# Feed-forward weight sums of pairs 1 to 5: added by GpSimd in place of VectorE

## The chip, the cores and the metric

The kernel runs on one core of a Trainium2 chip, in one launch. The metric is the device time of that core in microseconds (us); a lower time is better. Engines are named as in the profile: PE is TensorE (matmuls), PEld its weight loads, DVE is VectorE, ACT is ScalarE, POOL is GpSimd and SP is SyncE, which here only issues DMAs.

## The reference, cut to what matters

The reference is a two-layer streaming encoder on 512 tokens of width 1024, all in float32. Each layer has a mixer, a cross-attention to a memory and a gated feed-forward; a last RMSNorm ends it. The change lies in the feed-forward, which both layers have:

```python
D_FF = 256 * math.ceil(8 * D_MODEL / 3 / 256)   # 2816

def conv_ffn(xn, w_up, conv_w, conv_b, w_down):
    h = causal_depthwise_conv(xn @ w_up, conv_w) + conv_b
    g, u = jnp.split(h, 2, axis=-1)
    return (jax.nn.gelu(g) * u) @ w_down

x = x + conv_ffn(rms_norm(x, ffn_norm[layer]), ffn_w_up[layer], ffn_conv_w[layer], ffn_conv_b[layer], ffn_w_down[layer])
```

## The kernel before

**Tiling.** Tokens lie along the free dimension (512 columns), features on the 128 partitions. The product xn @ w_up has 44 blocks of 128 output features. Block p (of g) and block 22 + p (of u) form pair p, so each layer has 22 pairs, 0 to 21. Products are done in three matmuls of a high and a low part (`mm3`, lines 291 to 293: high by high, low by high, high by low), so every weight is split: ACT casts it to the high part (`wh`), DVE subtracts that from the original to get the low part (`wl`, all at line 282).

**Plain pairs and pairs of seven products.** Pair 0 goes through `plain`: two blocks of 24 matmuls on 512 columns. Pairs 1 to 21 (the tuple `SEVEN`) go through `seven`, a Strassen-like scheme with seven products of 12 matmuls on 256 columns instead of eight. It multiplies four forms of the tokens (made once per layer by `forms`, kept in `kv` tiles) and parts of the weights. Its weights per pair are: `f3`, the block of g as it is loaded (tile `raw`, 1024 columns); `f1`, the tile `sa`, where SP loads half of each block and a second DMA from POOL adds the block of u onto it in SBUF (line 1732, `accum_op=ALU.add`); `a22`, a part of u's block (tile `ra`, 512 columns); and two sums that an engine has to add. S2 = `sa[512:] + raw[:512]` goes to a tile `sb` (line 1753). After S2 has been split, S4 = `sb + raw[512:]` is added in place (line 1759) and split too. `sb` has two buffers, `sa` and `raw` three each.

**Behind the products.** The results are combined into `hs` (ACT copies at 1803 and 1810, DVE subtractions at 1793; ACT also keeps two intermediate results `u` at 1790 and seeds a PSUM bank at 1786). DVE then multiplies by the normalizer `rb` (1816). `tail` makes the convolution of three taps (ACT at 1669, DVE twice for each half at 1676), the gelu (ACT 1684), the product of g and u (DVE 1686) and the split of the activations (ACT 1690, DVE 282).

**The down projection.** w_down is taken in five chunks of pairs. From pair 5 on, `fill` puts two blocks `down` of a chunk that is ready into each pair: each is 12 matmuls on 512 columns with its own weight (tile `dr`) to be split. Pairs 1 to 4 have none, so there PE has the least work for each operation of DVE and ACT.

**What sets the order.** Nothing in the feed-forward is issued where it is written. `add(engine, duration, function, dependencies, due, take, free)` gives a task to the planner `Sched`, with a cost that is written into the program and a due time counted in PE time (`clock`). `Sched.run` goes through the tasks in the order of the costs and due times; each engine's queue is what comes out, and each engine works its queue in that order. S2's add is due 5 us before its pair, S4's 1.5 us before; splits are due 2 to 3 us before (plus an offset by product). For DVE the cost of 512 columns is `tt(512)`, 0.598 us. POOL has in this part of the program the accumulating DMAs and two small memsets of `hs`.

Of the kernel before, what the change touches and what calls it, by code (L numbers as in the profile page):

```python
# [14 lines left out]
ALU = mybir.AluOpType  # L15
# [50 lines left out]
class Plan:  # L66
# [11 lines left out]
    def add(self, fn, dur=0.0, deps=(), prio=None, take=(), free=(), chain=(), pre=(), after=0.0, order=(), load=(), st=None):  # L78
        it = Item(fn, dur, [d for d in deps if d is not None], len(self.items) if prio is None else prio, take, free, chain, pre, after, order, load, st)
        it.n = len(self.items)  # L80
        self.items.append(it)
        return it
# [154 lines left out]
class Builder:  # L237
# [1269 lines left out]
    def ffn_steps(self, layer, mp):  # L1507
# [3 lines left out]
        nc, t = self.nc, self.t  # L1511
        sc = Sched(raw=3, h=3, s2=1, s4=1, a22=1, sa=3, sb=2, ra=2, hs=2, c=1, dr=2, u2=1, u5=1, act=10, acc=2, y=2, s=2, w=2)
        add = sc.add
        tt = lambda n: 0.055 + 1.06e-3 * n
# [17 lines left out]
        def raw_tile(st, tag):  # L1532
            pool, n, bufs = RAWS[tag]
            st[tag] = self.til(pool, tag, (P, n), bufs=bufs)
            return st[tag]

        def load(st, tag, src, cols, at, dur=0.0017):
            def fn():
                to = raw_tile(st, tag)[:, :cols]
                nc.sync.dma_start(to.rearrange("p (a b) -> p a b", a=2) if len(src.shape) == 3 else to, src)  # L1540

            return add("SP", dur * cols, fn, (), at, [(tag, st)], (), 4.0)

        def parts(st, off=0):
            st["wh"], st["wl"] = self.parts(off)
# [177 lines left out]
        def seven(p, fill):  # L1723
            st, sa, sb, r2, f1, f3, s2, s4, a22 = ({} for _ in range(9))
            at = clock[0]
            A1, A2 = t["up"][layer, p], t["up"][layer, 22 + p]
            tt_ = nc.vector.tensor_tensor
            up2 = t["up"][layer].rearrange("(j p) r c -> p r j c", j=2)


            def onto(out, src, cols, deps, due):
                return add("POOL", 0.0029 * cols, lambda: nc.gpsimd.dma_start(out(), src(), accum_op=ALU.add), deps, due, (), (), 6.0)  # L1732

            SB = lambda: sb["sb"][:]
            soon = 40.0 if p < 5 else 0.0
            b1 = load(sa, "sa", up2[p][:, :, :512], 1024, at - 20.0 - soon, 0.0 if soon else 0.0017)
            b1 = onto(lambda: sa["sa"][:], lambda: A2, 1024, [b1], at - 16.0 - soon)
            l2 = load(r2, "raw", A1, 1024, at - 12.0)
            l1 = load(a22, "ra", A2[:, 512:], 512, at - 6.0)

            def small(s, tag):
                s["wh"], s["wl"] = small_(tag)

            def split(s, cols, deps, due, alloc, take, raw, free=()):
                def hi():
                    alloc()
                    nc.scalar.copy(s["wh"][:, :cols], raw())  # L1747

                h = add("ACT", act(cols), hi, deps, due - 3.0, take)
                return add("DVE", tt(cols), lambda: self.sub(s["wl"][:, :cols], raw(), s["wh"][:, :cols]), [h], due - 2.0, (), free)  # L1750

            def s2_():
                tt_(out=raw_tile(sb, "sb")[:], in0=sa["sa"][:, 512:], in1=r2["raw"][:, :512], op=ALU.add)

            b2 = add("DVE", tt(512), s2_, [b1, l2], at - 5.0, [("sb", sb)])
            w3 = split(f3, 1024, [l2], at, lambda: parts(f3, OFF), [("h", f3)], lambda: r2["raw"][:])
            w2 = split(s2, 512, [b2], at, lambda: small(s2, "s2"), [("s2", s2)], SB)
            w1 = split(f1, 1024, [b1], at + 1.0, lambda: parts(f1, OFF), [("h", f1)], lambda: sa["sa"][:])
            b4 = add("DVE", tt(512), lambda: tt_(out=SB(), in0=SB(), in1=r2["raw"][:, 512:], op=ALU.add), [w2], at - 1.5)
            w22 = split(a22, 512, [l1], at + 4.0, lambda: small(a22, "a22"), [("a22", a22)], lambda: a22["ra"][:], [("ra", a22)])  # L1760
            w4 = split(s4, 512, [b4], at + 5.0, lambda: small(s4, "s4"), [("s4", s4)], SB, [("sb", sb)])
            joined([w1, b2], at, [("sa", sa)])
# [533 lines left out]
```

## Time and profile before

| what | value |
|---|---|
| median of 3 runs | 1458.25 us (1457.26 to 1460.52) |
| the profiled execution | 1458.17 us |
| its span, first to last instruction | 1456.4 us |
| granted TensorE clock, mean | 0.999 |
| accumulating DMAs of the feed-forward on POOL | 42, 855 ns each to issue |
| pairs 1 to 5, layer 0 | about 417 to 475 us of the span |
| pairs 1 to 5, layer 1 | about 1120 to 1178 us of the span |

A row of the timeline has the start, the duration, the engine, the line, the operation, the tile written and the tiles read with their sizes, and in brackets how long the engine sat idle before it and what ended that. Consecutive operations on DVE overlap by some 0.08 us, so the distance of two starts, and not the duration, tells what one costs a gapless stream. A row of the waits has the time in total, how often, and the longest.

### The profile page before, as it was taken

What the parts mean: (1) busy time and instruction counts of PE and PEld (TensorE: products, weight loads), DVE (VectorE), ACT (ScalarE), POOL (GpSimd) and SP (SyncE); (2) the same over time, 40 slices, a digit from 0 to 9 for tenths busy, and PEclk for the clock granted to TensorE, in tenths of its full rate; (3) what the DMA queues carried; (4) which work ended last, traced back from release to release, by engine and by line L of the source; (5) the groups of instructions that cost most, each with busy time, mean ns of one, the idle gap of its engine ahead of it and who ended that gap; (6) DMA issues with size and microseconds to landing.
All of it is one profiled execution on the core that took longest, in us unless ns stands there. A gap on an engine that the chain in (4) does not pass through costs nothing.

```text
span 1456.4 us, 24072 instructions
## 1 busy us (share of the span) xinstructions
PE 1441.7 (99%) x9019; PEld 1279.8 (88%) x9019; DVE 1225.6 (84%) x2223; ACT 986.1 (68%) x1776; POOL 73.3 (5%) x116
## 2 busy tenths in 40 slices
PE   9999999999999999999999999999999999999998
PEld 7888787998899999999888888889988999999987
DVE  7789987867899988889669988887779998888974
ACT  7689666655677777777547665566566777777764
POOL 0001120000000000000000100000000000000000
PEclk9999999999999999999999999999999999999999
DMA  5222336752246666562233332656414666666422
GB/s 200 87 74 73 117 119 199 171 177 88 94 128 163 183 158 161 150 163 74 84 101 109 109 110 65 204 142 189 131 48 119 160 179 172 156 160 156 105 67 79
DMA packets 70628, 190.24 MB, mean 131 GB/s; under 512 B 7520, under 2 KB 7520, under 8 KB 70512
## 3 DMA queue, kind: packets, MB, share of 16 engines
q1 hardware_dynamic: 62736, 162.17, 35.1%
q0 software_dynamic: 7200, 26.22, 10.7%
q8 instruction: 70, 1.15, 0.3%
q14 instruction: 46, 0.38, 0.1%
q10 hardware_dynamic: 576, 0.33, 0.1%
HBM read 186.56 MB, written 2.13 MB: 130 GB/s over the span
## 4 chain that ended last, share of the span: by engine, by line
PE 82%; DVE 10%; ACT 4%; issue 2%; DMA 1%; POOL 0%; DVEq 0%; SPq 0%; POOLq 0%; ACTq 0%
PE acc L291 15%; PE acc L292 15%; PE acc L293 14%; PE w L293 6%; PE w L291 6%; PE w L292 6%; PE s L293 3%; PE s L291 3%; PE s L292 3%; PE acc L352 2%; PE acc L354 2%; PE acc L353 2%; DVE wl L282 2%; DMA sa<-in_xq_dram 1%; DVE x L771 1%
## 5 line engine op out<-in xcount | busy, mean ns | idle before, releaser
L282 DVE TENSOR_TENSOR wl<-raw,wh 128x1024 fp32r<-128x1024 f32 (+3 forms) x181 | 213.9, 1182 | 41.2 <-ACT wh L285 32.3
L291 PE MATMUL acc<-xh,wh 128*128 128x256 f32 (+1 forms) x624 | 206.8, 331 | 0.1
L293 PE MATMUL acc<-xh,wl 128*128 128x256 f32 (+1 forms) x624 | 205.7, 330 | 0.1
L292 PE MATMUL acc<-xl,wh 128*128 128x256 f32 (+1 forms) x624 | 205.5, 329 | 0.0
L285 ACT CAST wh<-raw 128x1024 fp32r<-128x1024 f32 (+1 forms) x123 | 126.6, 1034 | 84.6 <-PE acc L292 43.0
L1676 DVE SCALAR_TENSOR_TENSOR c<-hs,vec,c 128x512 f32<-128x512 f32 x176 | 130.5, 749 | 15.9 <-ACT c L1669 14.0
L291 PEld LDWEIGHTS acc<-xh,wh 128*128 128x128 f32 x624 | 117.2, 188 | 12.1 <-ACT v L1917 0.6
L293 PEld LDWEIGHTS acc<-xh,wl 128*128 128x128 f32 x624 | 117.1, 188 | 12.0 <-DVE wl L282 0.5
L292 PEld LDWEIGHTS acc<-xl,wh 128*128 128x128 f32 x624 | 117.2, 188 | 11.5
L293 PE MATMUL w<-ah,wl 128*128 128x512 f32 x304 | 119.1, 392 | 0.0
L292 PE MATMUL w<-al,wh 128*128 128x512 f32 x304 | 118.6, 390 | 0.0
L291 PE MATMUL w<-ah,wh 128*128 128x512 f32 x304 | 118.5, 390 | 0.0
L282 DVE TENSOR_TENSOR wl<-sa,wh 128x1024 fp32r<-128x1024 f32 x52 | 63.6, 1222 | 17.0 <-ACT wh L1747 15.6
L1669 ACT ACTIVATE c<-hs,vec 128x512 f32<-128x512 f32 x88 | 71.2, 816 | 9.6 <-DVE hs L1816 8.2
L1747 ACT CAST wh<-sa 128x1024 fp32r<-128x1024 f32 x42 | 44.0, 1049 | 35.4 <-PE w L292 30.4
L293 PEld LDWEIGHTS w<-ah,wl 128*128 128x128 f32 x304 | 57.1, 188 | 12.0
L291 PEld LDWEIGHTS w<-ah,wh 128*128 128x128 f32 x304 | 57.1, 188 | 10.0 <-ACT w L1584 0.2
L292 PEld LDWEIGHTS w<-al,wh 128*128 128x128 f32 x304 | 57.0, 188 | 9.8
L282 DVE TENSOR_TENSOR s<-sb,s 128x512 fp32r<-128x512 f32 x92 | 63.1, 686 | 2.2 <-ACT s L285 0.3
L1554 ACT CAST wh<-dr 128x512 fp32r<-128x512 f32 x64 | 39.7, 621 | 34.1 <-PE w L292 32.2
L1732 POOL DMA_DIRECT2D sa<-in_up_dram x42 | 35.9, 855 | 515.7 <-DMA sa<-in_up_dram 173.9
L291 PE MATMUL acc<-mem,wh 128*128 128x256 f32 (+1 forms) x192 | 61.5, 320 | 0.0
(534 smaller groups left out, 4667.8 us busy)
## 6 DMA issues: line engine op xcount, KB each, us to landing
raw<-in_up_dram SPq DMA_DIRECT2D x46, 512.0 KB, 3.5
sa<-in_up_dram SPq DMA_DIRECT2D x42, 512.0 KB, 4.3
sa<-in_up_dram POOLq DMA_DIRECT2D x42, 512.0 KB, 5.7
dr<-in_down_dram SPq DMA_DIRECT2D x64, 256.0 KB, 2.7
ra<-in_up_dram SPq DMA_DIRECT2D x42, 256.0 KB, 3.0
raw<-in_xk_dram SPq DMA_DIRECT2D x16, 512.0 KB, 3.6
raw<-in_wo_dram SPq DMA_DIRECT2D x16, 512.0 KB, 3.5
raw<-in_xv_dram SPq DMA_DIRECT2D x16, 512.0 KB, 3.4
```

The source lines that it names most:

```text
L282: self.nc.vector.tensor_tensor(out=lo, in0=v, in1=hi.bitcast(F32), op=ALU.subtract)
L285: self.nc.scalar.copy(hi, v)
L291: mm(out, wh, xh, start=first, stop=False, skip_group_check=parts)
L292: mm(out, wh, xl, start=False, stop=False, skip_group_check=parts)
L293: mm(out, wl, xh, start=False, stop=last, skip_group_check=parts)
L352: mm(ps, xh[k][:, ts], wh[:, ws], start=(k == 0), stop=False)
L353: mm(ps, xh[k][:, ts], wl[:, ws], start=False, stop=False)
L1554: nc.scalar.copy(st["wh"][:, :cols], st[tag][:, :cols])
L1669: nc.scalar.activation(st["c_"][:, j, :], hs()[:, j, 2:514], AF.Identity, scale=self.col("cw", (layer * 3 + 2) * 44 + blk), bias=self.col( ...
L1676: nc.vector.scalar_tensor_tensor(out=c, in0=hs()[:, j, n : n + 512], scalar=w, in1=c, op0=ALU.mult, op1=ALU.add)
L1732: return add("POOL", 0.0029 * cols, lambda: nc.gpsimd.dma_start(out(), src(), accum_op=ALU.add), deps, due, (), (), 6.0)
L1747: nc.scalar.copy(s["wh"][:, :cols], raw())
```

## The change

In pairs 1 to 5 of each layer the two adds S2 and S4 are issued on GpSimd (`nc.gpsimd.tensor_tensor`), and the planner is told that each takes 1.8 us there. In all other pairs they stay on VectorE. Operands, tiles and buffers are the same.

```diff
             tt_ = nc.vector.tensor_tensor
+            by_, add_ = (("POOL", 1.8), nc.gpsimd.tensor_tensor) if p in (1, 2, 3, 4, 5) else (("DVE", tt(512)), tt_)
...
             def s2_():
-                tt_(out=raw_tile(sb, "sb")[:], in0=sa["sa"][:, 512:], in1=r2["raw"][:, :512], op=ALU.add)
-
-            b2 = add("DVE", tt(512), s2_, [b1, l2], at - 5.0, [("sb", sb)])
+                add_(out=raw_tile(sb, "sb")[:], in0=sa["sa"][:, 512:], in1=r2["raw"][:, :512], op=ALU.add)
+
+            b2 = add(*by_, s2_, [b1, l2], at - 5.0, [("sb", sb)])
...
-            b4 = add("DVE", tt(512), lambda: tt_(out=SB(), in0=SB(), in1=r2["raw"][:, 512:], op=ALU.add), [w2], at - 1.5)
+            b4 = add(*by_, lambda: add_(out=SB(), in0=SB(), in1=r2["raw"][:, 512:], op=ALU.add), [w2], at - 1.5)
```

The added line moves the later ones down by one, so 1732 becomes 1733, 1753 becomes 1754, 1759 becomes 1760, 1793 becomes 1794 and 1816 becomes 1817 in the kernel after. As the planner has other costs, it also orders the tasks around the adds anew.

On POOL, at the start of layer 0's feed-forward, the queue before reads as follows (`sa` are the accumulating loads of pairs 1, 2, 3, then 4, 5, 6, 7; `hs` the two memsets):

```order
L1732 DMA sa_4593<-in_up_dram 128x1024
L1732 DMA sa_4595<-in_up_dram 128x1024
L1732 DMA sa_4597<-in_up_dram 128x1024
L1635 MEMSET hs_4587 128x2x2
L1635 MEMSET hs_4588 128x2x2
L1732 DMA sa_4693<-in_up_dram 128x1024
L1732 DMA sa_4885<-in_up_dram 128x1024
L1732 DMA sa_5038<-in_up_dram 128x1024
L1732 DMA sa_5175<-in_up_dram 128x1024
```

The same place in the queue after, with the adds of S2 (L1754) and S4 (L1760):

```order
L1733 DMA sa_4597<-in_up_dram 128x1024
L1754 TENSOR_TENSOR sb_4662<-sa_4593,raw_4603 128x512
L1754 TENSOR_TENSOR sb_4684<-sa_4595,raw_4635 128x512
L1760 TENSOR_TENSOR sb_4662<-sb_4662,raw_4603 128x512
L1635 MEMSET hs_4587 128x2x2
L1635 MEMSET hs_4588 128x2x2
L1754 TENSOR_TENSOR sb_4775<-sa_4597,raw_4660 128x512
L1733 DMA sa_4698<-in_up_dram 128x1024
L1760 TENSOR_TENSOR sb_4684<-sb_4684,raw_4635 128x512
L1733 DMA sa_4887<-in_up_dram 128x1024
L1754 TENSOR_TENSOR sb_4946<-sa_4698,raw_4721 128x512
L1760 TENSOR_TENSOR sb_4775<-sb_4775,raw_4660 128x512
```

The memsets now stand behind three adds, and from pair 4 on the accumulating loads alternate with adds of earlier pairs.

On DVE, in the same place of the program, the queue before has pair 1's and pair 2's S2 ahead of the last update of x (L619); `xl` is the low part of that x:

```order
L1753 TENSOR_TENSOR sb_4680<-sa_4593,raw_4603 128x512
L1753 TENSOR_TENSOR sb_4756<-sa_4595,raw_4635 128x512
L619 TENSOR_TENSOR x_145<-acc_900_4519,x_145 128x512
L282 TENSOR_TENSOR wl_4639<-raw_4603,wh_4638 128x1024
L604 SCALAR_TENSOR_TENSOR xl_912_4571<-x_145,vec,xh_911_4570 128x512
```

And after:

```order
L282 TENSOR_TENSOR s_947_4687<-sb_4662,s_947_4687 128x512
L619 TENSOR_TENSOR x_145<-acc_900_4519,x_145 128x512
L282 TENSOR_TENSOR wl_4639<-raw_4603,wh_4638 128x1024
L604 SCALAR_TENSOR_TENSOR xl_912_4571<-x_145,vec,xh_911_4570 128x512
L598 TENSOR_TENSOR sq_4329<-sq_4329,sqt_4574 128x512
```

The split of pair 1's S2 (`s`), which stood behind these rows before, now stands ahead of them, and both adds are gone from this queue.

Further on DVE, where pair 2 ends and pair 3 begins, the queue before reads (`c` and `al` belong to the tails, `a` is the split of A22, `hs_4588<-acc` a subtraction that PE's next product into that bank waits for):

```order
L1816 TENSOR_TENSOR hs_4587<-hs_4587,rb_4691 128x2x512
L1686 TENSOR_TENSOR c_4832<-c_4832 128x512
L282 TENSOR_TENSOR a_974_4888<-ra_4611,a_974_4888 128x512
L282 TENSOR_TENSOR s_977_4906<-sb_4775,s_977_4906 128x512
L282 TENSOR_TENSOR al_4925<-c_4832,ah_4924 128x512
L1759 TENSOR_TENSOR sb_4775<-sb_4775,raw_4660 128x512
L1793 TENSOR_TENSOR hs_4588<-acc_972_4865,u_978_4921 128x256
L1676 SCALAR_TENSOR_TENSOR c_4948<-hs_4587,vec,c_4948 128x512
L282 TENSOR_TENSOR wl_4941<-sa_4597,wh_4940 128x1024
```

And after:

```order
L1817 TENSOR_TENSOR hs_4587<-hs_4587,rb_4696 128x2x512
L1686 TENSOR_TENSOR c_4814<-c_4814 128x512
L282 TENSOR_TENSOR a_971_4869<-ra_4611,a_971_4869 128x512
L282 TENSOR_TENSOR s_975_4889<-sb_4684,s_975_4889 128x512
L282 TENSOR_TENSOR al_4908<-c_4814,ah_4907 128x512
L282 TENSOR_TENSOR s_979_4923<-sb_4775,s_979_4923 128x512
L1676 SCALAR_TENSOR_TENSOR c_4931<-hs_4587,vec,c_4931 128x512 x2
L1794 TENSOR_TENSOR hs_4588<-acc_973_4885,u_976_4905 128x256
L282 TENSOR_TENSOR wl_4950<-sa_4597,wh_4949 128x1024
```

S4's add is gone, a further split and two taps of the next tail stand ahead of the subtraction into `hs_4588`.

## The prediction

> **What bounds the kernel now.** The page's first part comes first, then the waits of the engine it points at.
>
> ```profile
> PE 1441.7 (99%) x9019; PEld 1279.8 (88%) x9019; DVE 1225.6 (84%) x2223; ACT 986.1 (68%) x1776; POOL 73.3 (5%) x116
> ```
>
> PE is busy for 99% of the span, so only time in which PE waits can be won. Its waits, longest first, name three releasers of the feed-forward's products:
>
> ```profile
> PE acc L291 <- DVE hs L1793: 1.0, 3, 0.3
> ...
> PE s L291 <- ACT u L1790: 0.8, 2, 0.4
> ...
> PE acc L291 <- ACT acc L1786: 0.5, 2, 0.3
> ```
>
> Next the windows over pairs 1 to 6 of both layers (columns: stretch, length, then PE, PEld, DVE, ACT, POOL busy, granted clock):
>
> ```profile
> 417.00:487.00 70.00, 68.83 (x549) 65.62 (x548) 68.29 (x106) 53.01 (x94) 5.13 (x6) 1.00 0.60 155
> 1120.00:1190.00 70.00, 68.97 (x549) 65.75 (x548) 68.28 (x106) 52.71 (x93) 5.14 (x6) 1.00 0.62 155
> ```
>
> PE lacks 70 - 68.83 = 1.17 us in layer 0 and 1.03 us in layer 1, at full granted clock. DVE is nearly as full. The timeline shows what a wait really costs, and the pace of the matmuls:
>
> ```profile
> 416.65 0.39 PE L292 MATMUL acc<-xl,wh 128*128 128x512 f32 x1
> 416.87 0.40 PE L293 MATMUL acc<-xh,wl 128*128 128x512 f32 x1
> 417.11 0.28 PE L291 MATMUL acc<-xh,wh 128*128 128x256 f32 x1
> ...
> 418.47 0.28 PE L291 MATMUL s<-kv,wh 128*128 128x256 f32 x1
> ...
> 426.52 0.28 PE L293 MATMUL acc<-xh,wl 128*128 128x256 f32 x1
> 427.14 0.39 PE L291 MATMUL acc<-kv,a 128*128 128x256 f32 x1 [0.34 <-DVE hs L1793]
> 427.36 0.28 PE L292 MATMUL acc<-kv,a 128*128 128x256 f32 x1
> ```
>
> A product of 12 narrow matmuls takes 418.47 - 417.11 = 1.36 us, so 0.113 us each by their starts. Around the wait two starts take 0.62 + 0.22 us where 0.23 would do: 0.61 us lost for 0.34 us that are called idle, 0.27 more. I count about six such gaps in each of the two windows, so PE loses some 1.17 + 6 x 0.27 = 2.8 us in layer 0 and 1.03 + 1.6 = 2.6 us in layer 1. That is the most that this change can win: **5.4 us**.
>
> Why is PE late there at all? From the DVE timeline in the same stretch, by the distance of starts:
>
> ```profile
> 424.54 0.42 DVE L1793 TENSOR_TENSOR hs<-s,u 128x256 f32<-128x256 f32 x1
> 424.87 0.74 DVE L1676 SCALAR_TENSOR_TENSOR c<-hs,vec,c 128x512 f32<-128x512 f32 x1
> 425.53 1.22 DVE L282 TENSOR_TENSOR wl<-sa,wh 128x1024 fp32r<-128x1024 f32 x1
> 426.67 0.42 DVE L1793 TENSOR_TENSOR hs<-acc,u 128x256 f32<-128x256 f32 x1
> ...
> 430.73 1.22 DVE L1816 TENSOR_TENSOR hs<-hs,rb 128x1024 f32<-128x1024 f32 x1
> 431.86 0.69 DVE L1686 TENSOR_TENSOR c<-c 128x512 f32<-128x512 f32 x1
> 432.46 0.69 DVE L282 TENSOR_TENSOR a<-ra,a 128x512 fp32r<-128x512 f32 x1
> 433.06 0.69 DVE L282 TENSOR_TENSOR s<-sb,s 128x512 fp32r<-128x512 f32 x1
> ```
>
> One pair asks of DVE: two 1024-wide splits at 1.14, one L1816 at 1.13, four taps (L1676) at 0.66, two L1793 at 0.33, and seven 512-wide operations at 0.60 (splits of S2, S4 and A22, the product L1686, the activations' split, and the two adds). That is 2.28 + 1.13 + 2.64 + 0.66 + 4.20 = 10.9 us. PE needs 7 x 1.36 = 9.5 us. DVE is short by 1.4 us in each of pairs 1 to 4, together 5.6 us, of which PE shows 2.8; the other **2.8 us** is lead that buffers and order hide. From pair 5 on two down blocks of 12 wide matmuls (0.23 us each by the starts above) lengthen PE's pair by 5.4 us and DVE catches up.
>
> **The change part by part.** Removed from DVE: 20 adds, ten in each layer.
>
> ```profile
> L1759 DVE TENSOR_TENSOR sb<-sb,raw 128x512 f32<-128x512 f32 x42 | 28.9, 688 | 0.7
> L1753 DVE TENSOR_TENSOR sb<-sa,raw 128x512 f32<-128x512 f32 x42 | 28.7, 688 | 0.6
> ```
>
> In DVE's gapless stream each is worth 0.60 us. By itself that turns 10.9 into 9.7 us a pair, nearly PE's pace.
>
> Added on POOL: 20 adds with two SBUF inputs. No row shows one. POOL's nearest rows have one input, and they show what happens when both engines want SBUF:
>
> ```profile
> 159.58 0.29 POOL L1009 TENSOR_SCALAR_AFFINE_SELECT tb<-ta 128x128 f32<-128x128 f32 x1 [8.65 <-DMA ta<-rows]
> 160.28 0.40 POOL L1009 TENSOR_SCALAR_AFFINE_SELECT tb<-ta 128x256 f32<-128x256 f32 x1 [0.40 <-DVE sm L778]
> ...
> 169.13 0.51 POOL L1009 TENSOR_SCALAR_AFFINE_SELECT tb<-ta 128x384 f32<-128x384 f32 x1 [0.54 <-DVE sm L778]
> ...
> 214.87 0.61 POOL L1009 TENSOR_SCALAR_AFFINE_SELECT tb<-ta 128x512 f32<-128x512 f32 x1 [3.50 <-DVE sm L771]
> ```
>
> ```profile
> 833.08 1.07 POOL L2006 TENSOR_SCALAR_AFFINE_SELECT mk<-mxb 128x512 f32<-128x512 f32 x2 [3.56 <-DVE a L466]
> ```
>
> ```profile
> 833.11 0.60 DVE L467 SCALAR_TENSOR_TENSOR y<-a,y 128x4 f32<-128x4 f32 x1
> ```
>
> ```profile
> L467 DVE SCALAR_TENSOR_TENSOR y<-a,y x21: 148/161/596, 272.8 to 980.3; 128x4 f32<-128x4 f32 x18, 128x2 f32<-128x2 f32 x3
> ```
>
> ```profile
> 174.93 1.21 DVE L282 TENSOR_TENSOR wl<-raw,wh 128x1024 fp32r<-128x1024 f32 x1
> 176.05 1.10 DVE L972 SCALAR_TENSOR_TENSOR ta<-ta,warm,nh 128x512 f32<-128x512 f32 x1
> ```
>
> ```profile
> 175.07 1.54 POOL L1009 TENSOR_SCALAR_AFFINE_SELECT tb<-ta 128x512 f32<-128x512 f32 x1 [1.95 <-DVE sm L778]
> ```
>
> POOL takes 0.11 us per 128 columns and 0.18 us beside, so 0.44 us of 0.62 passes over data at 512 columns. At 833.11 a DVE operation on 4 columns, with two SBUF inputs, lasts 596 ns instead of a median 161: held 0.435 us, until POOL is done. At 175.07 it is POOL that lasts 1.54 instead of 0.62 us, because a 1024-wide split with two SBUF inputs had begun first; the DVE operation behind that (176.05) then takes 1.10 us. So the two exclude each other, and nearly all of DVE's operations in pairs 1 to 4 read two SBUF tensors. A gapless DVE therefore pays for each POOL add with a stall h. Ends for h: 0.44 us, if two inputs pass as fast as one; 1.24 us, twice a whole one-input row. If the two inputs pass one after the other, the passes alone are 0.88. I take **h = 1.0 us**, between the last two.
>
> The Trainium skill has a rule on this that speaks against the change (SBUF — State Buffer, section "Who interferes with whom"): a VectorE instruction with two SBUF inputs and a GpSimd instruction that reads SBUF cannot run at once, and the one that starts first keeps the shared ports to its end. By that rule the trace agrees: 596 against 161 ns. The same skill gives (GPSIMD Engine Reference, section "Performance versus the Vector engine") a two-input add on GpSimd 1.96 times VectorE's time; an estimate from it is 1.96 x 0.60 = 1.18 us, with which the sum below would be 16 x 0.58 = +9.3 us. No run here shows that figure.
>
> The sum. A pair now costs DVE 10.9 - 1.2 + 2h = 11.7 us; it is short by 2.2 us, over pairs 1 to 4 by 8.8; less the 2.8 us of lead PE loses 6.0 us in place of 2.8. That is +3.2 us a layer, or in one formula for both layers 16 x (h - 0.60) = **+6.4 us**, never below -5.4. The adds of pair 5 (four in all) I cost at nothing: the down blocks' 5.4 us cover them; without that cover each would cost h - 0.60 too, +1.6 us together.
>
> The first adds of a layer move ahead. S2's split of pair 1 now stands on DVE in front of the last x update, and its cast on ACT in front of pair 1's first weight, both behind a POOL add. Queued behind them is the work that ends in this row, and PE reads its result at 410.73:
>
> ```profile
> 408.05 0.74 DVE L604 SCALAR_TENSOR_TENSOR xl<-x,vec,xh 128x512 fp32r<-128x512 f32 x1
> ```
>
> ```profile
> 410.73 0.39 PE L292 MATMUL acc<-xl,wh 128*128 128x512 f32 x1
> ```
>
> The slack is 410.73 - 408.79 = 1.9 us. DVE gets two adds less (-1.2), S2's split in front (+0.6) and up to three stalls (+3.0): +2.4 us, so at most 0.5 us shows on PE, and the eight adds of pairs 1 to 4 counted above already contain it. The two memsets of hs now stand behind three adds; the forms that wait for them have the same slack or more, so nothing.
>
> SWDGE loads share POOL's queue. In the new order pair 4's accumulating load stands behind pair 3's first add:
>
> ```profile
> 418.76 0.88 POOL L1732 DMA_DIRECT2D sa<-in_up_dram  x1 [13.52 <-DMA sa<-in_up_dram]
> ```
>
> ```profile
> sa<-in_up_dram POOLq DMA_DIRECT2D x42, 512.0 KB, 5.7
> ```
>
> ```profile
> 442.91 0.68 DVE L1753 TENSOR_TENSOR sb<-sa,raw 128x512 f32<-128x512 f32 x1
> ```
>
> Issued at 418.76 and landed 5.7 us later, it is first read at 442.91: 18 us of slack against adds of one or two us. On SP one load of sa in each layer goes one place later, which the same slack covers. Nothing for either; without that slack each load late would hold PE by its delay.
>
> **The rivals.**
> (a) DVE is really relieved: POOL's add holds it little or not at all. For it: 9.7 us a pair is almost PE's pace. Against it: the 596 ns row. With h = 0.42 or less 16 x 0.18 gives -2.9 us, with none the bound -5.4: 1455.3 down to 1452.8. Chance 0.20.
> (b) A wash: h between 0.42 and 0.78, when two inputs pass quicker than twice one. 1455.3 to 1461.1, the middle 1458. Chance 0.15.
> (c) Slower by latency as well: S4's add must wait for S2's split on DVE, then for a DVE operation in flight (up to 1.14 us), runs 1.24 instead of 0.60 us, and the cast behind it holds ACT's queue, so that u and acc copies for PE come late. It decides if S4's split is reached less than 1.8 us before its product. In pairs 1 to 4 of both layers about 1 us each on top: 6.4 + 8 = +14.4, or 1472.6. Against it: the planner was told 1.8 us for the add and puts S4's split further back. Chance 0.10.
>
> **How the numbers follow.** The profiled execution took 1458.17 us (span 1456.4), against a median of 1458.25, so the sum stands on 1458.2. Forecast: 1458.2 + 6.4 = 1464.6 us, chance 0.55; its own bounds are h = 0.78 (+2.9) and 1.24 (+10.2). About 0.2%, 2.9 us, is what a measurement of this kernel can tell from no change. Faster has (a), 0.20; same has (b), 0.15; slower has the forecast and (c), 0.65. The range reaches into (a) to 1455 and into (c) to 1471, and leaves out about 0.2.
>
> **What would show it.** Right: POOL's rows for L1754 and L1760 at 1.0 to 2.4 us, some twenty DVE operations in pairs 1 to 4 longer by about 1 us, DVE still gapless from 421 us, and PE's loss in the two windows grown to about 6 us each. Wrong: DVE's operations at their old lengths, idle time on DVE between pairs 2 and 4, or POOL's adds near 0.6 us. If instead PE waits for S4's split or for ACT copies behind an S4 cast, it was (c).

## The result, and the profile after

The changed kernel takes 1472.37 us (median of 5 runs, 1471.37 to 1472.52), the kernel before 1459.09 us beside it. The ratio is 1.009, 95% interval 1.0078 to 1.0102: **13.3 us slower**, where 6.4 were forecast. The profiled execution took 1472.52 us with a span of 1470.7.

First the busy times on the page of the changed kernel:

```profile
PE 1445.8 (98%) x9019; PEld 1282.3 (87%) x9019; DVE 1235.0 (84%) x2203; ACT 985.6 (67%) x1776; POOL 112.0 (8%) x136
```

DVE lost 20 instructions and is yet busy for 9.4 us longer than before. The 20 operations that left it are on POOL now. Their rows (minimum, median and maximum in ns):

```profile
L1754 POOL TENSOR_TENSOR sb<-sa,raw x10: 1512/2066/6417, 401.9 to 1153.5; 128x512 f32<-128x512 f32 x10
L1760 POOL TENSOR_TENSOR sb<-sb,raw x10: 1285/1574/1737, 408.7 to 1171.1; 128x512 f32<-128x512 f32 x10
```

The shortest add takes 1.285 us. The waits of PE name the same two releasers as before, with other amounts (us in total, times, longest):

```profile
PE acc L291 <- DVE hs L1794: 6.4, 8, 2.1
PE acc L291 <- ACT acc L1787: 4.6, 5, 1.3
```

They were 1.0 and 0.5 us. The windows over pairs 1 to 6 of the two layers show where (length, then PE, PEld, DVE, ACT and POOL busy, granted clock):

```profile
417.00:487.00 70.00, 64.71 (x505) 62.12 (x504) 67.52 (x94) 48.27 (x87) 20.15 (x12) 0.98 0.58 151
1120.00:1190.00 70.00, 64.56 (x481) 60.38 (x480) 67.49 (x91) 47.32 (x83) 16.64 (x13) 1.00 0.57 148
```

PE lacks 5.3 and 5.4 us of 70, where it lacked 1.2 and 1.0. By the distance of matmul starts, as in the prediction, it loses 9.3 us from 400 to 490 and 8.9 us in the same part of layer 1, against 2.9 and 2.6 before: 12.7 us more. Of the 14.4 us between the two profiled executions 1.7 are left, and most of that is pace: in these parts of the two layers some 390 narrow matmuls start 0.117 to 0.119 us after the one before, where some 80 did and 0.113 is usual, together 1.4 us. Why is not shown.

**Who is held.** The groups of the second taps of the convolution on DVE from 417 to 487 us, before and then after (busy, mean ns):

```profile
L1676 DVE SCALAR_TENSOR_TENSOR c<-hs,vec,c 128x512 f32<-128x512 f32 x24 | 17.8, 747 | 0.0
```

```profile
L1676 DVE SCALAR_TENSOR_TENSOR c<-hs,vec,c 128x512 f32<-128x512 f32 x23 | 22.6, 988 | 0.7 <-ACT c L1669 0.6
```

The taps take 0.24 us more each, 5.5 us in this window. At the start of the layer it is other operations, in the DVE timeline of the changed kernel:

```profile
402.18 2.19 DVE L282 TENSOR_TENSOR wl<-raw,wh 128x896 fp32r<-128x896 f32 x1
404.29 1.78 DVE L604 SCALAR_TENSOR_TENSOR xl<-x,vec,xh 128x512 fp32r<-128x512 f32 x1
...
409.13 1.93 DVE L282 TENSOR_TENSOR wl<-raw,wh 128x1024 fp32r<-128x1024 f32 x1
...
414.51 1.40 DVE L1497 TENSOR_TENSOR c<-hs,c 128x256 f32<-128x256 f32 x1
```

The same x update's row (L604) stood at 0.74 us, a 1024-wide split at 1.22. Each of the four stands beside one of POOL's first four adds. PE meets this at the `xl` of the last x update and, 11 us later, at a copy of ACT whose queue had waited for the normalizer's chain on DVE:

```profile
411.78 0.50 PE L292 MATMUL acc<-xl,wh 128*128 128x512 f32 x1 [0.22 <-DVE xl L604]
422.53 0.39 PE L291 MATMUL acc<-kv,s 128*128 128x256 f32 x1 [1.31 <-ACT acc L1787]
```

By starts these two cost 2.1 us, and 2.1 again in layer 1.

**Where POOL gets in.** POOL's timeline, then DVE's, in pair 4:

```profile
443.51 6.42 POOL L1754 TENSOR_TENSOR sb<-sa,raw 128x512 f32<-128x512 f32 x1 [3.69 <-DVE s L282]
```

```profile
444.01 1.22 DVE L282 TENSOR_TENSOR wl<-raw,wh 128x1024 fp32r<-128x1024 f32 x1
...
448.09 0.68 DVE L282 TENSOR_TENSOR s<-sb,s 128x512 fp32r<-128x512 f32 x1
449.06 3.55 DVE L1676 SCALAR_TENSOR_TENSOR c<-hs,vec,c 128x512 f32<-128x512 f32 x2 [0.28 <-ACT c L1669]
452.53 0.41 DVE L1794 TENSOR_TENSOR hs<-acc,u 128x256 f32<-128x256 f32 x1
```

For 4.8 us DVE runs splits and products back to back at their old lengths, and the add of S2 stands. It gets in when DVE itself waits, 0.28 us for ACT ahead of a tap; it ends at 449.93, S4's follows at 450.49, and two taps, 0.66 us each by the prediction's starts, take 3.55. Right behind them stands the subtraction that PE waits for:

```profile
453.00 0.39 PE L291 MATMUL acc<-kv,a 128*128 128x256 f32 x1 [2.08 <-DVE hs L1794]
```

A gap on DVE is not needed, though. In layer 1 the same add goes in ahead of a split whose start still overlaps the end of the tap before it (1153.32 + 0.74 against 1153.99), and it is the split that is held, 2.31 in place of 1.22 us:

```profile
1153.48 1.73 POOL L1754 TENSOR_TENSOR sb<-sa,raw 128x512 f32<-128x512 f32 x1 [3.69 <-DVE s L282]
```

```profile
1153.32 0.74 DVE L1676 SCALAR_TENSOR_TENSOR c<-hs,vec,c 128x512 f32<-128x512 f32 x1
1153.99 2.31 DVE L282 TENSOR_TENSOR wl<-raw,wh 128x1024 fp32r<-128x1024 f32 x1
```

Only 4 of the 20 adds go in at such a gap of 0.28 us. What decided otherwise here than at 443.51 is not shown.

**A second price of that wait.** The windows of 1 us behind it (PEclk is the value after POOL's busy time):

```profile
453.00:454.00 1.00, 1.00 (x6) 1.00 (x7) 1.00 (x2) 1.00 (x3) 0.00 (x0) 0.69 1.09 217
454.00:455.00 1.00, 1.00 (x6) 1.00 (x6) 1.00 (x4) 0.05 (x1) 0.00 (x0) 0.50 0.94 266
455.00:456.00 1.00, 1.00 (x6) 1.00 (x6) 1.00 (x3) 0.33 (x1) 0.00 (x0) 0.50 0.91 363
456.00:457.00 1.00, 1.00 (x8) 1.00 (x6) 1.00 (x2) 0.56 (x2) 0.00 (x0) 0.60 0.81 174
```

The granted clock falls to 0.50 for some 3.5 us: 0.31 + 0.50 + 0.50 + 0.40 = 1.7 us lost (1.6 by the distance of starts), in this execution in layer 0 alone. PE looks fully busy there, so no wait shows it.

### The profile page after: what moved, and what is told of

It is laid out like the page before. It is cut to its first block, busy times and chain, and to the rows that moved or that the text cites. A ratio compares the mean times of both kernels' runs of the same rounds, so it can differ in the third digit from the quotient of the medians.

```text
span 1470.7 us, 24050 instructions
## 1 busy us (share of the span) xinstructions
PE 1445.8 (98%) x9019; PEld 1282.3 (87%) x9019; DVE 1235.0 (84%) x2203; ACT 985.6 (67%) x1776; POOL 112.0 (8%) x136
## 4 chain that ended last, share of the span: by engine, by line
PE 72%; DVE 17%; issue 4%; ACT 4%; DMA 2%; SPq 0%; POOL 0%; DVEq 0%; POOLq 0%; ACTq 0%
PE acc L291 13%; PE acc L293 12%; PE acc L292 12%; PE w L293 6%; PE w L292 5%; PE w L291 5%; DVE wl L282 3%; PE s L291 3%; PE s L293 3%; PE s L292 3%; DVE c L1676 2%; PE acc L352 2%; PE acc L354 2%; PE acc L353 2%; DMA sa<-in_xq_dram 1%
## 5 line engine op out<-in xcount | busy, mean ns | idle before, releaser
L282 DVE TENSOR_TENSOR wl<-raw,wh 128x1024 fp32r<-128x1024 f32 (+3 forms) x181 | 218.8, 1209 | 39.8 <-ACT wh L285 32.3
L1676 DVE SCALAR_TENSOR_TENSOR c<-hs,vec,c 128x512 f32<-128x512 f32 x176 | 141.2, 807 | 17.8 <-ACT c L1669 15.5
L1669 ACT ACTIVATE c<-hs,vec 128x512 f32<-128x512 f32 x88 | 71.6, 816 | 17.2 <-DVE hs L1817 10.2
L291 PE MATMUL acc<-kv,a 128*128 128x256 f32 x200 | 57.2, 286 | 6.5 <-DVE hs L1794 6.4
```

The source lines that it names most:

```text
L282: self.nc.vector.tensor_tensor(out=lo, in0=v, in1=hi.bitcast(F32), op=ALU.subtract)
L291: mm(out, wh, xh, start=first, stop=False, skip_group_check=parts)
L1669: nc.scalar.activation(st["c_"][:, j, :], hs()[:, j, 2:514], AF.Identity, scale=self.col("cw", (layer * 3 + 2) * 44 + blk), bias=self.col( ...
L1676: nc.vector.scalar_tensor_tensor(out=c, in0=hs()[:, j, n : n + 512], scalar=w, in1=c, op0=ALU.mult, op1=ALU.add)
```

## The experiments

The theory: POOL's read of SBUF holds DVE for about 1 us per add, and PE waits for what stands behind the held operation (**hold**). The rivals: the new order of the tasks costs (**order**); the sums are ready later, as in rival (c) (**latency**); or the planner's ignorance of the hold does it. Costs below are differences of medians against the kernel before on the same chip.

One thing has to be known for reading them. If an add is issued on another engine while the planner is told the same as in the changed kernel, rows on DVE and ACT, in some runs on PE too, still change place; what moves them was not examined. Runs in which POOL keeps an instruction in the add's place (write only, one input, halves) have the queues of PE, DVE and ACT of the kernel that they are compared with, row for row. These are the clean comparisons.

**1. The planner's new costs, adds on VectorE.** PE's queue is that of the changed kernel, DVE's and ACT's partly.

```diff
-            by_, add_ = (("POOL", 1.8), nc.gpsimd.tensor_tensor) if p in (1, 2, 3, 4, 5) else (("DVE", tt(512)), tt_)
+            by_, add_ = (("POOL", 1.8), tt_) if p in (1, 2, 3, 4, 5) else (("DVE", tt(512)), tt_)
```

> The order of the kernel after (the planner still believes in 1.8 us on POOL), but the twenty adds are issued on DVE. Stall theory (each POOL add holds DVE about 1.1 us, and that is the whole loss): no stalls, DVE back at 10.9 us a pair, so about the time before, 1458 to 1461 us. Order theory (part of the loss is that the new order leaves the subtractions into hs behind two taps and has no lead): 1462 to 1466 us. Latency theory (PE waits for the chain split, POOL add, cast, split): 1457 to 1460, since the chain is short again.

1458.19 us, ratio 1.0002 (0.9992 to 1.0011). PE's new order costs nothing, and with it the order theory's 1462 to 1466 is out, as far as DVE's and ACT's queues allow the comparison.

**2. The adds on POOL, the planner told VectorE's 0.6 us.**

```diff
-            by_, add_ = (("POOL", 1.8), nc.gpsimd.tensor_tensor) if p in (1, 2, 3, 4, 5) else (("DVE", tt(512)), tt_)
+            by_, add_ = (("DVE", tt(512)), nc.gpsimd.tensor_tensor) if p in (1, 2, 3, 4, 5) else (("DVE", tt(512)), tt_)
```

> The planner is told that the adds run on DVE at 0.6 us, so its order is nearly that of the kernel before, but the twenty adds are issued on POOL. Stall theory: DVE at 10.9 - 1.2 + 2 x 1.1 = 11.9 us a pair, 16 x 0.5 = +8 us: 1464 to 1469 us. Order theory: below the kernel after by the part that its order costs, 1464 to 1467 us. Latency theory: worse than after, since S4's split stands directly behind its add: 1474 us or more.

1477.44 us, ratio 1.0132 (1.0116 to 1.0147): +19.6 us, where the stall theory alone had 1464 to 1469; it lies in the latency theory's range, 1474 or more. So the 1.8 us that the planner is told are worth 6 us, as far as this run's other order allows the comparison: without them the sums come too late for their users. Here ACT's casts do wait for POOL's S4; in the changed kernel no wait of PE, DVE or ACT names a POOL add, so there latency has no part that its waits show. PE's longest waits are for L1794 in both:

```profile
ACT s L1748 <- POOL sb L1760: 7.9, 5, 3.2
```

```profile
PE acc L291 <- DVE hs L1794: 11.0, 10, 2.0
```

**3. Write only.** POOL fills the sum's tile with two memsets and reads nothing. The sums S2 and S4 of pairs 1 to 5 are left out.

```diff
+            def twice(out, in0, in1, op):
+                for _ in range(2):
+                    nc.gpsimd.memset(out, 0.01)
...
+            by_, add_ = (("POOL", 1.8), twice) if p in (1, 2, 3, 4, 5) else (("DVE", tt(512)), tt_)
```

> Same order and queues as after, but each POOL add is replaced by two POOL memsets of the same tile, which read nothing from SBUF (the sums S2 and S4 of pairs 1 to 5 are left out). Stall theory: DVE is not held and keeps 9.7 us a pair, PE's loss nearly goes: 1453 to 1457 us, and no DVE operation is longer than in the kernel before. Latency theory: the chain through POOL is nearly as long, 1464 to 1472 us. Order theory: 1455 to 1460 us.

1457.23 us, ratio 0.9997 (0.9987 to 1.0006), just above the stall theory's 1453 to 1457 and far below the latency theory's 1464. Its page, its largest waits in the feed-forward (the added lines move the later ones by four, so L1791 and L1798 are L1787 and L1794 of the changed kernel), and the taps from 417 to 487 us:

```profile
PE 1440.4 (99%) x9019; PEld 1279.2 (88%) x9019; DVE 1216.5 (83%) x2203; ACT 984.0 (68%) x1776; POOL 94.4 (6%) x156
```

```profile
PE acc L291 <- ACT acc L1791: 1.9, 4, 0.7
PE acc L291 <- DVE hs L1798: 0.6, 2, 0.3
```

```profile
L1676 DVE SCALAR_TENSOR_TENSOR c<-hs,vec,c 128x512 f32<-128x512 f32 x24 | 17.7, 741 | 0.7 <-ACT c L1669 0.6
```

This run decides. PE, DVE and ACT have the queues of the changed kernel and POOL works at the same places, for 1.1 us a sum against the add's 1.3 undisturbed; only the read is gone, and with it 13.3 + 0.6 = 13.9 us. (A memset does not wait for the loads of what it replaces either, but in the changed kernel no add waited for a load: POOL's idle time ahead of them ended with PE or with a split on DVE. On SP six pairs of neighbouring loads change places; in both kernels no wait of PE, DVE or ACT names a load from 395 to 700 and from 1100 to 1410 us.) The taps are at 741 ns. The Trainium skill says so (SBUF — State Buffer, section "Who interferes with whom": VectorE's second SBUF input meets a GpSimd instruction that reads SBUF, and not one that only writes); by that rule the trace agrees, 741 against 988 ns.

The run shows a second thing: DVE is relieved of 20 adds for nothing in return, and the kernel gains 0.6 us, which is within its error. DVE's busy time falls by 9.1 us, but PE's waits in the feed-forward have only moved to copies of ACT: 1.9 + 0.6 = 2.5 us in the rows above, where the three rows of the kernel before made 1.0 + 0.8 + 0.5 = 2.3.

**4. One input.** POOL copies `raw` to the sum's tile; the sums are left out again.

```diff
+            def copied(out, in0, in1, op):
+                nc.gpsimd.tensor_copy(out, in1)
...
+            by_, add_ = (("POOL", 1.8), copied) if p in (1, 2, 3, 4, 5) else (("DVE", tt(512)), tt_)
```

> Same order as after, but each POOL add is replaced by a POOL copy of its second input: one SBUF input (the sums are left out). Stall theory: DVE is held about 0.45 to 0.6 us for each, so 16 x (0.5 - 0.6): 1455 to 1460 us, between the write-only kernel and the kernel after. Latency theory: in proportion to POOL's time, 1460 to 1466 us. Order theory: 1459 to 1463 us.

1459.70 us, ratio 1.0011 (1.0001 to 1.0021): +1.9 us. The queues of PE, DVE and ACT are the same, and DVE is busy for 4.6 us longer than in run 3:

```profile
PE 1441.8 (99%) x9019; PEld 1280.1 (88%) x9019; DVE 1221.1 (84%) x2203; ACT 984.2 (67%) x1776; POOL 98.5 (7%) x136
```

So a one-input read holds DVE for 0.23 us on average and costs 2.5 us against run 3.

**5 and 6. Eight adds in pairs 1 and 2, twelve in pairs 3 to 5.** The tuple is `(1, 2)` and `(3, 4, 5)`.

> Only pairs 1 and 2 of each layer add on POOL, eight adds in all, most of them at a layer's start. Place theory (what an add costs depends on what DVE does next: at the start of a layer the chain of the normalizer and the last x are behind it; in pairs 2 to 5 the subtraction into hs that PE waits for): the two losses at the start and the one in pair 2 stay, 2 x 2.6 us: 1462 to 1465 us. Sum theory (16 x (h - 0.6), any add alike): 8 x 0.5 = +4, less what pairs 3 and 4 hide: 1459 to 1462 us.

> Only pairs 3, 4 and 5 of each layer add on POOL, twelve adds in all; the start of a layer is as in the kernel before but for pair 3's first add. Place theory: the waits for the subtractions in pairs 3 and 4 stay, with or without the half clock behind the longest: 1462 to 1468 us. Together with the pairs 1 and 2 alone about the whole of after's +13. Sum theory: 8 to 12 adds x 0.5 = +4 to 6, of which the 2.8 us of lead a layer may hide all: 1457 to 1461 us.

1463.98 us, ratio 1.0038 (1.0025 to 1.0051), and 1469.27 us, ratio 1.0073 (1.0058 to 1.0088): +5.2 and +10.5 us, 0.65 and 0.87 us an add. Both parts cost, and together (15.7) a little more than the whole. The start of the layer is in the first alone: there PE loses 1.6 us at `xl` and at the first `acc` copy, and in the second kernel nothing before 426 us. The latter goes beyond its expected range.

**7. The same adds where DVE has room: pairs 8 to 12,** where it is busy for 132.5 of 150 us before.

```diff
-            by_, add_ = (("POOL", 1.8), nc.gpsimd.tensor_tensor) if p in (1, 2, 3, 4, 5) else (("DVE", tt(512)), tt_)
+            by_, add_ = (("POOL", 1.8), nc.gpsimd.tensor_tensor) if p in (8, 9, 10, 11, 12) else (("DVE", tt(512)), tt_)
```

> Pairs 8 to 12 of each layer add on POOL in place of pairs 1 to 5: twenty adds where each pair has two down blocks and DVE idles 2 to 3 us of 15. Cover theory: nothing is lost, 1457 to 1460 us, although each add still holds DVE about 1.1 us. Place theory without cover (an add is let in just before an operation that PE needs): 2 to 6 us slower, 1460 to 1464 us.

1469.06 us, ratio 1.007 (1.0055 to 1.0085): +10.3 us. That cover would make them free is refuted, and the time also lies beyond the 1460 to 1464 of the other theory. The chain in pair 8, on DVE, ACT and PE:

```profile
493.71 1.78 DVE L1676 SCALAR_TENSOR_TENSOR c<-hs,vec,c 128x512 f32<-128x512 f32 x1
```

```profile
495.53 0.63 ACT L1684 ACTIVATE c<-c 128x512 f32<-128x512 f32 x1 [1.96 <-DVE c L1676]
496.06 0.60 ACT L1748 CAST s<-sb 128x512 fp32r<-128x512 f32 x1
496.57 0.36 ACT L1791 COPY u<-acc 128x256 f32<-128x256 f32 x1
```

```profile
496.99 0.38 PE L291 MATMUL acc<-kv,wh 128*128 128x256 f32 x1 [1.35 <-ACT u L1791]
```

The tap is held by the add at 492.74, the gelu on ACT waits 1.96 us for it, and behind the gelu in ACT's queue stands the copy that PE needs. Idle time that DVE has later does not help: PE needs single results, not DVE's total.

**8. The hold written into the plan,** as 1.1 us of DVE per add.

```diff
             b2 = add(*by_, s2_, [b1, l2], at - 5.0, [("sb", sb)])
+            if by_[0] == "POOL":
+                add("DVE", 1.1, None, [b1, l2], at - 5.0)
...
+            if by_[0] == "POOL":
+                add("DVE", 1.1, None, [w2], at - 1.5)
```

> As after, but the planner also books 1.1 us of DVE time, without an instruction, for each add on POOL, so its order reckons with 11.9 us a pair on DVE. If after loses because its order does not know of the stalls: 1462 to 1467 us. If it loses because POOL is let in only where DVE's stream breaks, which no booked time changes: 1469 to 1474 us.

1475.41 us, ratio 1.0111 (1.0095 to 1.0128): +16.6 us, no better than without, and above both ranges. Booked in this way, knowledge of the hold does not help; the queues are others here, so no more can be said.

**9. Pairs 8 to 12, write only,** with run 7's queues on PE, DVE, ACT and SP.

```diff
+            by_, add_ = (("POOL", 1.8), twice) if p in (8, 9, 10, 11, 12) else (("DVE", tt(512)), tt_)
```

> Pairs 8 to 12 again, but GpSimd writes the tile of each sum with two memsets of 512 columns and reads nothing (the sums S2 and S4 of these pairs are left out). The queues of PE, DVE, ACT and SP are those of the run with the adds in pairs 8 to 12. Hold theory: the 10.3 us of that run come from DVE operations that a reading GpSimd holds, so they go: 1457 to 1460 us. Order and latency theory: they come from the new order on ACT and from sums that are ready later, which memsets of about the same length keep: 1464 to 1470 us.

1460.05 us, ratio 1.0009 (0.9999 to 1.0018): +2.0 us, at the upper edge of the hold theory's range. Of run 7's 10.3 us 8.3 go with the read; order and latency have at most 2.0.

**10. As much more work for DVE, and no hold.** Each add stays on VectorE, with a second operation of 512 columns behind it.

```diff
+            def longer(out, in0, in1, op):
+                tt_(out=out, in0=in0, in1=in1, op=op)
+                tt_(out=out, in0=out, in1=out, op=ALU.max)
...
+            by_, add_ = (("POOL", 1.8), longer) if p in (1, 2, 3, 4, 5) else (("DVE", tt(512)), tt_)
```

> Pairs 1 to 5, the planner told POOL as in the changed kernel, but each add is issued on VectorE with a second operation of 512 columns behind it that changes nothing (the maximum of the sum with itself). DVE gets 20 x 0.60 = 12 us more work, about what the holds gave it net, and no operation of it is held. Balance theory: what counts is DVE's total in pairs 1 to 4, 16 x 0.60 = 9.6 us more: 1467 to 1470 us. Place theory: what counts is that a hold falls on the taps right ahead of a subtraction that PE waits for, while ordinary work of DVE stands where it is covered: 1459 to 1464 us.

1465.86 us, ratio 1.0049 (1.0033 to 1.0066): +7.8 us, between both ranges, and with a queue of its own on PE. DVE is busy for 11.5 us more than in run 1 (1225.6):

```profile
PE 1445.3 (99%) x9019; PEld 1281.4 (88%) x9019; DVE 1237.1 (84%) x2243; ACT 985.8 (67%) x1776; POOL 74.0 (5%) x116
```

The view that only the place of a hold counts was too strong: DVE time taken by plain work in these pairs costs too, here two thirds of itself (7.8 of 11.5 us). As PE's queue is another, the two thirds are not a clean figure.

**11. S2's adds alone on POOL.**

```diff
-            b4 = add(*by_, lambda: add_(out=SB(), in0=SB(), in1=r2["raw"][:, 512:], op=ALU.add), [w2], at - 1.5)
+            b4 = add("DVE", tt(512), lambda: tt_(out=SB(), in0=SB(), in1=r2["raw"][:, 512:], op=ALU.add), [w2], at - 1.5)
```

> Pairs 1 to 5, only the ten adds of S2 on GpSimd, those of S4 on VectorE. Hold theory, each add the same: half of 13.3 us, 1464 to 1467 us. Chain theory (rival c: S4's add waits for S2's split and passes its lateness on to ACT's queue): the cost sits in S4, 1458 to 1462 us here.

1465.40 us, ratio 1.0044 (1.0028 to 1.006): +7.3 us by medians, half of the whole for half of the adds, and in the hold theory's range. S4's chain is not needed for the cost; as the queues are others, a small price of it is not excluded.

**12. Each add in two halves of 256 columns,** in the queues of the changed kernel.

```diff
+            def halves(out, in0, in1, op):
+                for h in (slice(0, 256), slice(256, 512)):
+                    nc.gpsimd.tensor_tensor(out=out[:, h], in0=in0[:, h], in1=in1[:, h], op=op)
...
+            by_, add_ = (("POOL", 1.8), halves) if p in (1, 2, 3, 4, 5) else (("DVE", tt(512)), tt_)
```

> As the changed kernel, but each add on GpSimd is issued as two of 256 columns; the queues of PE, DVE, ACT and SP are the same. Total theory: the two holds together are as long as one or longer, and what counts is their sum: 1471 to 1476 us. Length theory: what counts is the longest single hold in front of a subtraction that PE waits for, and GpSimd gets in at more places, each for half as long: 1462 to 1469 us.

1469.45 us, ratio 1.0069 (1.0051 to 1.0086): +11.4 us by medians, between the two ranges and inside neither. DVE's busy time lies between those of run 3 and of the changed kernel:

```profile
PE 1444.8 (98%) x9019; PEld 1281.2 (87%) x9019; DVE 1231.8 (84%) x2203; ACT 985.5 (67%) x1776; POOL 121.5 (8%) x156
```

No half add held POOL longer than 1.73 us, and PE's longest wait for the subtraction into `hs` (L1794 of the changed kernel) is 1.0 in place of 2.1 us, but it waits for ACT more often. Which of the two theories holds stays open.

**Hold against cost.** The runs in the same queues with and without a read give the dependence. The hold is the difference of DVE's busy times, the cost that of the costs:

| run | against | hold, us | cost, us | us per us |
|---|---|---|---|---|
| one input, pairs 1 to 5 | write only | 1221.1 - 1216.5 = 4.6 | 1.9 + 0.6 = 2.5 | 0.5 |
| halves, pairs 1 to 5 | write only | 1231.8 - 1216.5 = 15.3 | 11.4 + 0.6 = 12.0 | 0.8 |
| the changed kernel | write only | 1235.0 - 1216.5 = 18.5 | 13.3 + 0.6 = 13.9 | 0.75 |

A whole add holds DVE for 18.5 / 20 = 0.93 us. None of the runs is faster than the kernel before by more than its error, and run 3 shows that a relief of DVE in these pairs had next to nothing to give.

## Why the prediction was right in its direction and short in its size

**PE bounds, and DVE is nearly full in pairs 1 to 4: right**, and the waits grew on the lines named. That at most 5.4 us could be won was right as a bound and useless as a credit (below).

**The stall h = 1.0 us: right.** 0.93 us on average in the table, and 1.0 to 1.1 in single rows (404.29: 1.78 against 0.74). The 596 ns row had shown the mechanism. The estimate of 1.18 us for the add itself, from the Trainium skill's ratio of 1.96 (GPSIMD Engine Reference, section "Performance versus the Vector engine"), is near the shortest row, 1.285; DVE's hold is less than the add's length.

**The sum, 16 x (h - 0.60): the step that failed.** With the measured h it would say 16 x 0.33 = +5.3 us, with its own upper bound of 1.24 +10.2, so h is not what was wrong. It gives each add that leaves DVE a credit of 0.60 us and each us of stall a price of 1. Run 3, with the relief and no hold, should by it have reached the floor, -5.4; it measured -0.6. Run 4 should have gained too, and cost 1.9. The credit is not there, because PE's next wait is for ACT. The price is 0.75 in place of 1, but for 20 adds and not 16. So the balance is 20 x 0.93 x 0.75 - 0.6 = 13.3 us. This is worked back from the runs; beforehand the row to ask was that of the waits for ACT, two of the three quoted. The lead of 2.8 us that the prediction took off its shortage was treated as a constant; the first us of hold did cost less than the later ones (0.5 against 0.75), but not nothing.

**By place the misses are three.** (1) The start of the layer was put at no more than 0.5 us and called contained in the sum; the rows show 2.1 us in each layer, 4.2 together. The 1.9 us of slack was counted for `xl` alone, and the normalizer's chain to ACT's queue, where 1.6 of the 2.1 are lost, was not followed. (2) That a wait of 2 us on PE lowers the clock was not foreseen: 1.7 us. (3) The adds of pair 5 were costed at nothing since DVE has time there; runs 7 and 9 show that 20 adds with such cover still cost 8.3 us. The first two leave 12.7 - 4.2 - 1.7 = 6.8 us for pairs 2 to 6, near the forecast 6.4 by luck: a credit too large and a price too high cancelled.

**The loads on POOL's queue, SP and the memsets: nothing, as costed.** The waits of PE name none of them.

**The rivals.** (a) and (b) fell with h. (c) gave 1472.6, and the time is 1472.4, but by another mechanism: no engine waits for a POOL add, and no S4 split and no copy behind an S4 cast is what PE waits for at the long waits; S2 alone costs half (run 11), and write-only sums cost nothing in the same queues (run 3). Part of (c) is true all the same: a hold does pass through ACT's queue to PE (422.53 here, 496.99 in run 7), and run 2 shows what later sums cost when the planner does not allow for them.

**What would show it:** POOL's rows were to be 1.0 to 2.4 us, and 6.42 was the exception, an add that starved. The longer operations on DVE and PE's loss were there (9.3 and 8.9 in place of 6 us). DVE was gapless but for some short waits, such as the 0.28 us at 449.06.

## What to carry to other kernels

An engine's relief is worth nothing until the next wait behind it is looked at, while a hold on the same engine costs most of its length (here 0.75 of it), so the two are not to be set off one against the other in one formula. An add on GpSimd that reads SBUF beside a VectorE stream with two SBUF inputs costs VectorE more (0.93 us) than doing the add there (0.60 us), and slack in VectorE's total does not hide it if the operation held is one whose result is on its way to PE. The cheap test is to replace the moved instruction by one of like length that reads nothing, in the same queue: it separates order, occupancy and contention in one run.

## What the runs showed of the hardware that was not expected

A gapless DVE stream of operations with two SBUF inputs can keep a reading POOL out for microseconds, but not for good. The add at 443.51 took 6.42 us in place of 1.29 and went in at a gap; its counterpart in layer 1 took 1.73 without one. In run 2 the same add took 6.86 us and went in with no gap at all, ahead of a tap that starts before the split ahead of it has ended:

```profile
444.20 6.86 POOL L1754 TENSOR_TENSOR sb<-sa,raw 128x512 f32<-128x512 f32 x1 [5.14 <-DVE s L282]
```

```profile
448.72 1.21 DVE L282 TENSOR_TENSOR wl<-sa,wh 128x1024 fp32r<-128x1024 f32 x1
449.86 1.75 DVE L1676 SCALAR_TENSOR_TENSOR c<-hs,vec,c 128x512 f32<-128x512 f32 x1
```

In the changed kernel and runs 2, 5 to 8 and 11, while an add of more than 1.8 us stood (up to 1.35 us before its end), only TENSOR_TENSOR operations started on DVE, never a SCALAR_TENSOR_TENSOR such as a tap; whether that is a rule was not tested. In run 12 an add of 256 columns took 0.725 us at the least.

PE's granted clock fell to 0.50 for some 3.5 us after idle times of 2.08 us (layer 0 here) and 1.95 us (run 2, layer 1), and stayed at 1.00 after 1.93 and 1.89 us (run 2, layer 0). The rows of run 2, first where it fell, then where it stayed:

```profile
1163.80 0.39 PE L291 MATMUL acc<-kv,a 128*128 128x256 f32 x1 [1.95 <-DVE hs L1794]
```

```profile
1165.00:1166.00 1.00, 1.00 (x6) 1.00 (x6) 1.00 (x3) 0.99 (x2) 0.00 (x0) 0.50 0.74 123
```

```profile
452.00 0.39 PE L291 MATMUL acc<-kv,a 128*128 128x256 f32 x1 [1.93 <-DVE hs L1794]
```

```profile
453.00:454.00 1.00, 1.00 (x11) 1.00 (x10) 1.00 (x2) 0.78 (x2) 0.18 (x1) 1.00 0.93 164
```

The Trainium skill puts the idle time that lowers the clock at about 3.4 us (TensorE: Matmul & The Clock Gate, section "Part 1: The HAM clock gate"); here some 2 us were enough in two of the four cases, and the measurement decides.
